# mLSTM head states of both directions in one array, built by zero-padded keys in the pass of the head before

## The chip, the cores and the metric

One core of one Trainium2 chip runs the whole layer. The metric is the device time in microseconds (us) of one execution of the program. The five engines are TensorE (PE; its weight loads are shown as PEld), VectorE (DVE), ScalarE (ACT), GpSimd (POOL) and SyncE (SP); SP issues all DMA transfers of this kernel from one queue, in order.

## The reference, cut to what matters

The layer projects a sequence of 2048 positions, mixes it with two groups of 8 heads each (gated DeltaNet, and mLSTM), and projects back. Everything is float32. The change is in the mLSTM group. Each head runs over the sequence forwards and backwards; in one direction and chunkwise it computes

```python
def step(carry, inp):
    c_state, n_state, m_state = carry
    ...
    num = inter[..., None] * jnp.einsum('bhld,bhde->bhle', q_c, c_state) + jnp.einsum('bhts,bhse->bhte', w_intra, v_c)
    den = inter * jnp.einsum('bhld,bhd->bhl', q_c, n_state) + jnp.sum(w_intra, axis=-1)
    h = num / jnp.maximum(jnp.abs(den), jnp.exp(-m_t))[..., None]
    ...
    c_state = carry_dec[..., None, None] * c_state + jnp.einsum('bhld,bhle->bhde', wk, v_c)
    n_state = carry_dec[..., None] * n_state + jnp.sum(wk, axis=2)
```

A key or query has 64 entries, a value 128. A column of ones behind the values (129 columns, VW) makes n_state and den by the same products as c_state and num.

## The kernel before, in words

The sequence is cut into NC = 16 chunks of 128 positions, and into NB = 4 blocks of CB = 4 chunks. The program has four stages that follow each other, each with pools of its own in SBUF and PSUM: the gates and the first projections; the inversion for the DeltaNet heads woven with the mLSTM projections (m_k, m_q, m_v); the DeltaNet scan; and the mLSTM stage (from line 1188), after which the output projection is finished. In the mLSTM stage PE also does the first half of the output projection for 14 chunks (`ahead`, line 1173, with `product`, line 1161), as filler between the steps of the heads.

Ahead of the mLSTM stage. `gates` makes per-position decay factors; `dec` (line 492) holds the factor by which a state is multiplied from chunk to chunk, for the 16 pairs of direction and head. `m_k` (line 740) transposes the keys, scales them for each direction into `tk` and stores them; `m_v` (line 770) stores the values with their column of ones. Both go into one DRAM array per head, `mwv_d`, whose row of a chunk has 128 entries of keys (64 for each direction) and then 129 of values. So a store writes runs of 512 or 516 bytes, with the other's bytes between them.

The mLSTM stage. `states(h)` (line 1206) walks t = 0 to 15: it loads a block of keys and values together (`wv`, line 1212; 6 buffers), multiplies keys by values in one matmul (`pc`, line 1225; 128 rows of the result: 64 forwards, 64 backwards, for the same chunk t), makes the forward state with one DVE instruction (line 1231), and copies the backward half by ACT into the state array (line 1237). The array `C` has two slots for each chunk, one per direction, with zeros in the half of the partitions that belongs to the other direction. For head h + 1 these steps run inside the pass of head h, one per item; for head 0 they run by themselves at the start of the stage. `pc` has one buffer in PSUM (pool `ps_c`), so the next `pc` waits until both DVE and ACT have read the last.

The pass of a head (`core`, line 1299) takes the chunks from 15 down to 0, an item for each. In an item come, in this order: the backward state of the chunk, in place, by DVE (line 1314); the masking of the next block on POOL every fourth item (`mask_block`, line 1265: two selects on `rb`, and the scaling of the queries `qe`, line 1277); the weights of the next item (`weights`: matmul `pq`, two exponentials on ACT, one product on DVE); one step of `states` for the next head; a stretch of filler; then the matmuls into `pn`: scaled queries times both states in one matmul of 258 columns (line 1335), and weights times values for each direction (line 1339); then the division (lines 1342 to 1346), the sum of the directions (lines 1348 and 1349), and again filler. `load_block` (line 1240) loads keys, queries, `rb` and `qe` two blocks ahead; `qe` is one transfer from two rows of `in_d`, each spread over 64 partitions (line 1259).

The order of PE and of POOL in this stage is the order in which the program is written (`manual_schedule`, line 1363). The other queues (DVE, ACT, SP) are ordered by the framework's planner, which goes by its own model of time; a transfer into a pool is planned no earlier than a buffer of its tag comes free.

## Time and profile before

| what | before |
|---|---|
| median of 3 runs | 2766.45 us (2766.29 to 2770.05) |
| profiled execution, its own time | 2766.64 us |
| its span, first to last instruction | 2764.9 us |
| mean granted TensorE clock | 0.977 of full speed |
| PE, PEld busy | 2574.2 us, 2146.5 us |
| DVE, ACT, POOL busy | 1688.9 us, 1254.8 us, 948.8 us |
| mLSTM stage, first to last of its matmuls | 2112 to 2551 us of the span |

How to read the profile: a busy PE is a PE that has matmuls in flight, not one at its peak. A float32 matmul is two passes, which the trace lists as two instructions; the fillers are one pass. "Idle before" is the time for which an engine had nothing to run, and the arrow names what ended it. The granted clock is given as a share of full speed; its two levels are 1.2 and 2.4 GHz.

### The profile page before, as it was taken

What the parts mean: (1) busy time and instruction counts of PE and PEld (TensorE: products, weight loads), DVE (VectorE), ACT (ScalarE), POOL (GpSimd) and SP (SyncE); (2) the same over time, 40 slices, a digit from 0 to 9 for tenths busy, and PEclk for the clock granted to TensorE, in tenths of its full rate; (3) what the DMA queues carried; (4) which work ended last, traced back from release to release, by engine and by line L of the source; (5) the groups of instructions that cost most, each with busy time, mean ns of one, the idle gap of its engine ahead of it and who ended that gap; (6) DMA issues with size and microseconds to landing.
All of it is one profiled execution on the core that took longest, in us unless ns stands there. A gap on an engine that the chain in (4) does not pass through costs nothing. (4 is left out here: it accounts for less than half of the span.)

```text
span 2764.9 us, 48198 instructions
## 1 busy us (share of the span) xinstructions
PE 2574.2 (93%) x16494; PEld 2146.5 (78%) x16494; DVE 1688.9 (61%) x4176; ACT 1254.8 (45%) x3400; POOL 948.8 (34%) x1410
## 2 busy tenths in 40 slices
PE   7999999999999998999999999999995788889998
PEld 5788878788887776777788888888884677778887
DVE  5547776677768887887425555555554565666333
ACT  6356666666652333433333333333333555555321
POOL 2136665666653232333211111111112333333133
PEclk9999999999999999999999999999997899999999
DMA  4135555655553545454556656666656677775564
GB/s 150 56 101 176 173 168 152 181 157 186 175 181 114 142 117 152 119 150 123 138 158 200 212 183 212 198 211 209 201 172 181 203 211 205 204 208 156 191 190 156
DMA packets 437343, 468.09 MB, mean 169 GB/s; under 512 B 31306, under 2 KB 302570, under 8 KB 437098
## 3 DMA queue, kind: packets, MB, share of 16 engines
q1 hardware_dynamic: 437097, 465.01, 56.3%
q8 instruction: 131, 2.15, 0.3%
q14 instruction: 115, 0.93, 0.1%
HBM read 301.92 MB, written 162.99 MB: 168 GB/s over the span
## 5 line engine op out<-in xcount | busy, mean ns | idle before, releaser
L272 PE MATMUL acc<-hh,wh 128*128 128x512 f32 x2048 | 834.3, 407 | 0.0
L272 PE MATMUL acc<-hl,wh 128*128 128x512 f32 x2048 | 827.6, 404 | 0.0
L272 PE MATMUL acc<-hh,wl 128*128 128x512 f32 x2048 | 822.7, 402 | 0.0
L272 PEld LDWEIGHTS acc<-hh,wl 128*128 128x128 f32 x2048 | 388.6, 190 | 72.8 <-issue 1.0
L272 PEld LDWEIGHTS acc<-hh,wh 128*128 128x128 f32 x2048 | 389.3, 190 | 70.3 <-issue 1.2
L272 PEld LDWEIGHTS acc<-hl,wh 128*128 128x128 f32 x2048 | 389.4, 190 | 69.1 <-issue 1.0
L230 POOL TENSOR_TENSOR wl<-wr,wh 128x256 fp32r<-128x256 f32 x256 | 206.0, 818 | 611.0 <-ACT wh L229 485.0
L579 DVE SCALAR_TENSOR_TENSOR cacc<-raw,gcw,cacc 128x512 f32<-128x512 f32 x256 | 213.4, 860 | 78.1 <-POOL raw L595 37.8
L1167 PE MATMUL po<-woh,ch 128*128 128x512 f32 x512 | 212.6, 416 | 17.6 <-ACT woh L1143 15.6
L150 POOL TENSOR_TENSOR rs<-rs,mhalf 128x4 f32<-128x4 f32 x64 | 64.3, 1010 | 477.0 <-DVE rs L147 232.5
L1167 PE MATMUL po<-wol,ch 128*128 128x512 f32 x512 | 209.7, 410 | 1.4 <-POOL wol L1144 1.4
L1167 PE MATMUL po<-woh,cl 128*128 128x512 f32 x512 | 208.6, 408 | 0.0
L229 ACT CAST wh<-wr 128x256 fp32r<-128x256 f32 (+1 forms) x260 | 98.0, 403 | 235.1 <-DMA wr<-in_w_in_dram 154.1
L710 POOL COPY dg<-T 32x128 f32<-32x128 f32 x256 | 151.9, 593 | 16.6 <-DVE T L700 6.6
L700 DVE SCALAR_TENSOR_TENSOR T<-pk,sc,E 128x256 f32<-128x256 f32 x256 | 109.6, 474 | 47.5 <-PE pk L697 39.6
L874 POOL COPY Z<-ZD 32x256 f32<-32x256 f32 x128 | 92.0, 719 | 123.8 <-DMA Z<-uq_d 68.6
L579 DVE SCALAR_TENSOR_TENSOR cacc<-raw,mcw,cacc 128x512 f32<-128x512 f32 x128 | 100.8, 805 | 52.4 <-POOL raw L595 27.1
L579 DVE SCALAR_TENSOR_TENSOR kq<-raw,gcw,kq 128x512 f32<-128x512 f32 x128 | 104.8, 824 | 33.0 <-ACT kq L575 24.0
L1167 PEld LDWEIGHTS po<-woh,ch 128*128 128x128 f32 x512 | 98.4, 192 | 32.8 <-ACT woh L1143 17.1
L1225 PE MATMUL pc<-wv 128*128 128x129 f32 x256 | 56.9, 317 | 66.8 <-DMA wv<-mwv_d 53.7
L1167 PEld LDWEIGHTS po<-wol,ch 128*128 128x128 f32 x512 | 98.6, 193 | 16.6 <-POOL wol L1144 3.4
L1029 DVE SCALAR_TENSOR_TENSOR sn<-sn,eGL,ps 128x128 f32<-128x128 f32 x224 | 68.0, 344 | 71.1 <-PE ps L1024 71.1
(603 smaller groups left out, 4892.1 us busy)
## 6 DMA issues: line engine op xcount, KB each, us to landing
kv<-kv_d SPq DMA_DIRECT2D x256, 256.0 KB
wr<-in_w_in_dram SPq DMA_DIRECT2D x256, 128.0 KB
uq_d<-T SPq DMA_DIRECT2D x64, 512.0 KB
uq<-uq_d SPq DMA_DIRECT2D x128, 256.0 KB
wv<-mwv_d SPq DMA_DIRECT2D x32, 514.0 KB
zg_d<-zt SPq DMA_DIRECT2D x64, 256.0 KB
E<-grow_d SPq DMA_DIRECT2D x64, 256.0 KB
kv_d<-tk SPq DMA_DIRECT2D x64, 256.0 KB
```

The costliest lines, as they stand in the source:

```text
L150: nc.gpsimd.tensor_tensor(out=rs, in0=rs, in1=mhalf[:, :CB], op=ALU.pow)
L229: nc.scalar.copy(out=hi, in_=raw[:, :, :n])
L230: nc.gpsimd.tensor_tensor(out=lo, in0=raw[:, :, :n], in1=hi.bitcast(F32), op=ALU.subtract)
L272: nc.tensor.matmul(ps, l[:, k % KH, :], r[b][:, k, :], start=(k == 0 and i == 0), stop=(k == KC - 1 and i == 2),)
L579: nc.vector.scalar_tensor_tensor(out=acc, in0=raw[:, t : t + TB], scalar=cw[:, t * n_ct + ct : t * n_ct + ct + 1], in1=acc, op0=ALU.mult, ...
L700: nc.vector.scalar_tensor_tensor(out=T2[d][:, :, i], in0=pk, scalar=sc[:, u, c : c + 1], in1=E[d][:, i].unsqueeze(1).broadcast_to([P, 2, P ...
L710: nc.gpsimd.tensor_copy(out=dg[qs, :, at : at + CB], in_=T2[d][qs, 1, :, qs].rearrange("p c i -> p i c"),)
L874: nc.gpsimd.tensor_copy(out=self.Z[bs, :, :, bs], in_=ZD[bs].rearrange("p x (d c) -> p d c x", d=2)[:, :, self.qs],)
L1029: nc.vector.scalar_tensor_tensor(out=sn[d], in0=st[d], scalar=eGL[:, u, c : c + 1], in1=ps[d][:, 2], op0=ALU.mult, op1=ALU.add,)
L1167: nc.tensor.matmul(po, l[:, i, :], r[:, ns], start=(first and i == 0 and j == 0), stop=(last and i == H - 1 and j == 2),)
L1225: nc.tensor.matmul(pc, wv[:, t % CB, 0:P], wv[:, t % CB, P:], start=True, stop=True)
```

## The change

The states of both directions are made in the pass ahead, by the same instruction. `C` has one slot per step (half the size): slot t holds, in its upper and lower halves of the partitions, the forward state before chunk t and the backward state before chunk 15 - t. For this `pc` is now the sum of two matmuls: the forward keys of chunk t with its values, and the backward keys of chunk 15 - t with its values. Keys are spread into tiles with 64 zeros between the two directions (`wks`), so that a window of 128 columns has the keys of one direction and zeros for the other; POOL spreads them from a staged load. The one DVE instruction then works on 128 partitions, the ACT copy (line 1237) and the in-place backward step (line 1314) are gone, and the step with t = 15 makes no matmul. `dec` is reordered to fit, by 17 POOL copies in `gates`. The scaled queries become two tiles of 128 partitions, each zero in one half, and the matmul of 258 columns becomes two of 129. Keys and values have their own DRAM arrays and loads. Each step of `states` now yields twice: its matmuls stand where they stood, its DVE instruction is emitted later in the item, between lines 1348 and 1349.

```diff
-    mwv_d = [dram.tile([P, NC, 2 * P + 1], F32, name=f"mwv_d{h}") for h in range(H)]
+    mwk_d = [dram.tile([P, NC, 2, 64], F32, name=f"mwk_d{h}") for h in range(H)]
+    mv_d = [dram.tile([P, NC, P + 1], F32, name=f"mv_d{h}") for h in range(H)]
...
-            nc.scalar.activation(out=dec, in_=t2, func=AF.Exp)
+            nc.scalar.activation(out=t2, in_=t2, func=AF.Exp)
+            nc.gpsimd.tensor_copy(out=dec[0:64], in_=t2[0:64, :H])
+            for c in range(NC):
+                nc.gpsimd.tensor_copy(out=dec[64:128, :, c], in_=t2[64:128, H:, NC - 1 - c])
...
-                    nc.sync.dma_start(
-                        out=mwv_d[h][:, cs, 0:P], in_=tk.rearrange("p c d k -> p c (d k)")
-                    )
+                    nc.sync.dma_start(out=mwk_d[h][:, cs], in_=tk)
...
-                nc.sync.dma_start(
-                    out=mwv_d[h][:, b * CB : (b + 1) * CB, P : 2 * P + 1], in_=tk
-                )
+                nc.sync.dma_start(out=mv_d[h][:, b * CB : (b + 1) * CB], in_=tk)
...
-            Cs = [ms.tile([P, NC, 2, VW], F32, name=f"C{i}", bufs=1) for i in range(2)]
+            Cs = [ms.tile([P, NC, VW], F32, name=f"C{i}", bufs=1) for i in range(2)]
             for C in Cs:
-                nc.vector.memset(C[0:64, 0, 0, :], 0.0)
-                nc.vector.memset(C[64:128, NC - 1, 1, :], 0.0)
-                nc.gpsimd.memset(C[0:64, :, 1, :], 0.0)
-                nc.gpsimd.memset(C[64:128, :, 0, :], 0.0)
+                nc.vector.memset(C[:, 0, :], 0.0)
...
+            qes = [ms.tile([P, 2, TB], F32, name=f"qe{i}", bufs=1) for i in range(3)]
+            for qe in qes:
+                nc.gpsimd.memset(qe[64:128, 0, :], 0.0)
+                nc.gpsimd.memset(qe[0:64, 1, :], 0.0)
+            wks = [ms.tile([P, CB, 3, 64], F32, name=f"wk{i}", bufs=1) for i in range(NB)]
+            for wk in wks:
+                nc.gpsimd.memset(wk[:, :, 1, :], 0.0)
+            vs, blk, staged = {}, {}, {}
+            def wk_of(h, b):
+                return wks[b if h % 2 == 0 else (1, 0, 3, 2)[b]]
+            def load_keys(h, blocks):
+                for b in blocks:
+                    t = ms.tile([P, CB, 2, 64], F32, tag="wt", name="wt", bufs=NB)
+                    nc.sync.dma_start(out=t, in_=mwk_d[h][:, b * CB : (b + 1) * CB])
+                    staged[h, b] = t
+            def spread_keys(h, blocks):
+                for b in blocks:
+                    nc.gpsimd.tensor_copy(out=wk_of(h, b)[:, :, ::2, :], in_=staged.pop((h, b)))
+            def load_values(h, blocks):
+                for b in blocks:
+                    vs[h, b] = ms.tile([P, CB, VW], F32, tag="v", name="v", bufs=2 * NB)
+                    nc.sync.dma_start(out=vs[h, b], in_=mv_d[h][:, b * CB : (b + 1) * CB])
...
+                outer, inner = (0, 3), (1, 2)
                 if h == 0:
-                    for b in range(NB):
-                        load(b)
+                    for bs in (outer, inner):
+                        load_keys(0, bs)
+                        load_values(0, bs)
+                        spread_keys(0, bs)
                 for t in range(NC):
-                    if h > 0 and t % CB == 0:
-                        load(t // CB)
...
-                    nc.tensor.matmul(
-                        pc, wv[:, t % CB, 0:P], wv[:, t % CB, P:], start=True, stop=True
-                    )
+                    if h > 0 and t == 0:
+                        load_values(h, inner)
+                        spread_keys(h, inner)
+                    if h + 1 < H and t == NC // 2:
+                        load_keys(h + 1, outer)
+                        load_values(h + 1, outer)
+                    if h + 1 < H and t == NC - CB:
+                        spread_keys(h + 1, outer)
+                        load_keys(h + 1, inner)
+                    if t < NC - 1:
...
+                        for d, c in enumerate((t, NC - 1 - t)):
+                            b, i = c // CB, c % CB
+                            nc.tensor.matmul(
+                                pc, wk_of(h, b)[:, i].rearrange("p s k -> p (s k)")[:, d * 64 : d * 64 + P],
+                                vs[h, b][:, i, :], start=(d == 0), stop=(d == 1),
+                            )
+                    yield
                     if t == 0:
-                        nc.vector.tensor_copy(out=C[0:64, 1, 0, :], in_=pc[0:64])
+                        nc.vector.tensor_copy(out=C[:, 1, :], in_=pc)
                     elif t < NC - 1:
                         nc.vector.scalar_tensor_tensor(
-                            out=C[0:64, t + 1, 0, :], in0=C[0:64, t, 0, :],
-                            scalar=dec[0:64, h, t : t + 1], in1=pc[0:64],
+                            out=C[:, t + 1, :], in0=C[:, t, :], scalar=dec[:, h, t : t + 1], in1=pc,
                             op0=ALU.mult, op1=ALU.add,
                         )
-                    if t > 0:
-                        nc.scalar.copy(out=C[64:128, t - 1, 1, :], in_=pc[64:128])
                     yield
...
-                nc.sync.dma_start(
-                    out=qe,
-                    in_=in_d[h : h + H + 1 : H, bs].unsqueeze(1).broadcast_to([2, 64, TB]),
-                )
+                qe = qes[j % 3]
+                for d in range(2):
+                    nc.sync.dma_start(
+                        out=qe[d * 64 : (d + 1) * 64, d, :],
+                        in_=in_d[d * H + h, bs].partition_broadcast(64),
+                    )
...
-                qv = qe.rearrange("p (c i) -> p c i", i=P)
-                nc.gpsimd.tensor_tensor(out=qv, in0=qv, in1=kq[:, :, 1, :], op=ALU.mult)
+                for d in range(2):
+                    hs = slice(d * 64, (d + 1) * 64)
+                    qv = qe[hs, d, :].rearrange("p (c i) -> p c i", i=P)
+                    nc.gpsimd.tensor_tensor(out=qv, in0=qv, in1=kq[hs, :, 1, :], op=ALU.mult)
...
-                    if c < NC - 2:
-                        nc.vector.scalar_tensor_tensor(
-                            out=C[64:128, c, 1, :], in0=C[64:128, c + 1, 1, :],
-                            scalar=dec[64:128, H + h, c + 1 : c + 2], in1=C[64:128, c, 1, :],
-                            op0=ALU.mult, op1=ALU.add,
-                        )
...
-                    nc.tensor.matmul(
-                        pn, qe[:, i * P : (i + 1) * P], C[:, c], start=True, stop=False
-                    )
-                    for d in range(2):
-                        nc.tensor.matmul(pn[:, d], W[:, d], v, start=False, stop=(d == 1))
+                    for d, slot in enumerate((c, NC - 1 - c)):
+                        nc.tensor.matmul(
+                            pn[:, d], qe[:, d, i * P : (i + 1) * P], C[:, slot, :],
+                            start=True, stop=False,
+                        )
+                        nc.tensor.matmul(pn[:, d], W[:, d], v, start=False, stop=True)
...
                     nc.scalar.activation(out=oc, in_=pn[:, 0, :P], func=AF.Copy, scale=dn[:, 0:1])
+                    next(following, None)
```

## Rows read from the trace of the kernel before

**Rows 1.** Page, part 1: engine, busy us, share of the span, instructions.
```profile
PE 2574.2 (93%) x16494; PEld 2146.5 (78%) x16494; DVE 1688.9 (61%) x4176; ACT 1254.8 (45%) x3400; POOL 948.8 (34%) x1410
```

**Rows 2.** Windows: stretch, length, busy of each engine, PEclk, DMA share, GB/s.
```profile
2100.00:2120.00 20.00, 7.40 (x31) 6.50 (x32) 4.72 (x14) 3.85 (x15) 3.17 (x4) 0.54 0.89 231
...
2325.00:2375.00 50.00, 40.19 (x224) 34.81 (x222) 30.85 (x104) 25.27 (x86) 13.51 (x15) 0.93 0.69 200
```

**Rows 3.** Waits of PE from 2175 to 2510: us in total, times, longest.
```profile
PE pc L1225 <- DMA wv<-mwv_d: 29.5, 12, 3.6
PE pc L1225 <- ACT C L1237: 9.4, 13, 1.7
```

**Rows 4.** Timeline of PE: start, us, line, tiles, count [idle before, and its releaser].
```profile
2175.26 0.60 PE L1335 MATMUL pn<-C,qe 128*128 128x258 f32 x2
...
2185.62 0.60 PE L1335 MATMUL pn<-C,qe 128*128 128x258 f32 x2
...
2316.58 0.60 PE L1335 MATMUL pn<-C,qe 128*128 128x258 f32 x2
2317.01 0.61 PE L1339 MATMUL pn<-wv,W 128*128 128x129 f32 x4
...
2318.15 0.38 PE L1285 MATMUL pq<-kq 128*128 128x128 f32 x2
2318.37 0.39 PE L1225 MATMUL pc<-wv 128*128 128x129 f32 x2
...
2330.19 0.77 PE L1225 MATMUL pc<-wv 128*128 128x129 f32 x2 [3.50 <-DMA wv<-mwv_d]
...
2507.85 0.60 PE L1335 MATMUL pn<-C,qe 128*128 128x258 f32 x2
...
2529.05 0.60 PE L1335 MATMUL pn<-C,qe 128*128 128x258 f32 x2
...
2538.57 0.60 PE L1335 MATMUL pn<-C,qe 128*128 128x258 f32 x2
```

**Rows 5.** Timeline of SP, the queue that issues transfers: start, us to issue.
```profile
2097.01 0.56 SPq L1253 DMA_DIRECT2D rb<-rv_d  x1
2097.62 0.56 SPq L1259 DMA_DIRECT2D qe<-in_d  x1
...
2318.18 3.02 SPq L1212 DMA_DIRECT2D wv<-mwv_d  x1
```

**Rows 6.** Timeline at the start of the mLSTM stage, POOL and PE.
```profile
2102.76 0.63 POOL L1271 TENSOR_SCALAR_AFFINE_SELECT rb<-rb 128x512 f32<-128x512 f32 x1 [4.61 <-DMA rb<-rv_d]
...
2109.96 1.26 POOL L1277 TENSOR_TENSOR qe<-qe,kq 128x512 f32<-128x512 f32 x1 [6.56 <-DMA qe<-in_d]
...
2112.46 7.88 PE L1225 MATMUL pc<-wv 128*128 128x129 f32 x32 [17.57 <-DMA wv<-mwv_d]
```

**Rows 7.** Groups by line, 2175 to 2510: busy us, mean ns | idle before, releasers.
```profile
L1335 PE MATMUL pn<-C,qe 128*128 128x258 f32 x210 | 65.3, 393 | 0.9 <-DVE o L1349 0.9
L1314 DVE SCALAR_TENSOR_TENSOR C<-C,dec 64x129 f32<-64x129 f32 x88 | 36.8, 418 | 3.5 <-ACT C L1237 0.7
L1277 POOL TENSOR_TENSOR qe<-qe,kq 128x512 f32<-128x512 f32 x27 | 35.2, 1305 | 0.0
L1231 DVE SCALAR_TENSOR_TENSOR C<-C,dec,pc 64x129 f32<-64x129 f32 x92 | 30.9, 336 | 24.7 <-PE pc L1225 24.5
L1237 ACT COPY C<-pc 64x129 f32<-64x129 f32 x99 | 25.9, 262 | 33.8 <-DVE C L1231 31.8
L1342 DVE TENSOR_TENSOR dn<-pn,em 128x2 f32<-128x2 f32 x105 | 16.4, 156 | 39.7 <-PE pn L1339 38.9
```

**Rows 8.** Waits from 860 to 1420, of DVE and of PE.
```profile
DVE tk L752 <- DMA mwv_d<-tk: 16.1, 11, 3.0
...
PE pt L604 <- ACT cacc L584: 21.2, 7, 5.9
```

**Rows 9.** Timeline of POOL behind the gates.
```profile
165.53 1.44 POOL L230 TENSOR_TENSOR wl<-wr,wh 128x256 fp32r<-128x256 f32 x2 [19.42 <-ACT wh L229]
```

More of the change, by code (lines that the diff above doesn't have):

```diff
@@ L107 @@
     wkc = cols.tile([P, U, NC], F32, name="wkc")
-    dec = cols.tile([P, U, NC], F32, name="dec")
+    dec = cols.tile([P, H, NC], F32, name="dec")
     em = cols.tile([P, U, NC], F32, name="em")
@@ L1206, in states @@
+            def load_values(h, blocks):
+                for b in blocks:
+                    vs[h, b] = ms.tile([P, CB, VW], F32, tag="v", name="v", bufs=2 * NB)
+                    nc.sync.dma_start(out=vs[h, b], in_=mv_d[h][:, b * CB : (b + 1) * CB])
             def states(h):
                 C = Cs[h % 2]
-                def load(b):
-                    wvs[h, b] = ms.tile([P, CB, P + VW], F32, tag="wv", name="wv", bufs=6)
-                    nc.sync.dma_start(out=wvs[h, b], in_=mwv_d[h][:, b * CB : (b + 1) * CB, :])
+                outer, inner = (0, 3), (1, 2)
@@ L1214, in states @@
                 if h == 0:
-                    for b in range(NB):
-                        load(b)
+                    for bs in (outer, inner):
+                        load_keys(0, bs)
+                        load_values(0, bs)
+                        spread_keys(0, bs)
                 for t in range(NC):
-                    if h > 0 and t % CB == 0:
-                        load(t // CB)
-                    wv = wvs[h, t // CB]
-                    if h == 0 and t % 3:
-                        pc = ps_n.tile([P, 2, VW], F32, tag="pn", name="pc")[:, 0]
-                    else:
-                        pc = ps_c.tile([P, VW], F32, tag="pc", name="pc")
@@ new lines, in states @@
+                    if t < NC - 1:
+                        if h == 0 and t % 3:
+                            pc = ps_n.tile([P, 2, VW], F32, tag="pn", name="pc")[:, 0]
+                        else:
+                            pc = ps_c.tile([P, VW], F32, tag="pc", name="pc")
+                        for d, c in enumerate((t, NC - 1 - t)):
[4 more added lines that the diff above has]
+                            )
@@ L1303, in core @@
                 load_block(0)
-                for _ in states(0):
-                    yield
+                for i, _ in enumerate(states(0)):
+                    if i % 2:
+                        yield
                 mask_block(0)
@@ L1332, in core @@
                     i = c % CB
[L1333 removed]
+                    qe, v = blk[h, b][1], vs[h, b][:, i, :]
                     pn = ps_n.tile([P, 2, VW], F32, tag="pn", name="pn")
[L1335 to L1339 removed]
+                    for d, slot in enumerate((c, NC - 1 - c)):
[4 more added lines that the diff above has]
+                        nc.tensor.matmul(pn[:, d], W[:, d], v, start=False, stop=True)
                     dn = ms.tile([P, 2], F32, tag="dn", name="dn")
```

3 lines of the change are left out of this document (removed).

## The prediction

> **What bounds the kernel now.** I read the busy shares first: PE 93%, DVE 61%, ACT 45%, POOL 34% [rows 1]. That would say that more matmuls cost their full length and that work taken from DVE and ACT gives nothing. The share is a mean over four stages, though, so I read the stage that the change touches. In the windows of the mLSTM stage PE is busy 40.2 of 50 us, at 0.93 of its clock, DVE 30.9, ACT 25.3, POOL 13.5, the transfers 0.69 [rows 2]: no engine is full there. So the third view is what PE waits for in the regular part, from 2175 to 2510: 29.5 us in 12 waits of pc for the block wv of keys and values, and 9.4 us in 13 waits of pc for the ACT copy that still holds its one PSUM buffer [rows 3]. Nothing else there is near them.
>
> The timeline of PE gives the price of an item without waits. From 2175.26 to 2185.62 four items take 10.36 us, 2.59 each, and PE goes from one matmul to the next. The pn matmuls of the stretch number 105 (210 passes [rows 7]), from 2175.26 to 2507.85, so 104 items take 332.6 us, 3.20 each [rows 4]. At 10.36 for four they would take 269.4; 63.2 us are lost, of which the two waits are 38.9. The other 24.3 are PE at the lower clock behind waits (0.93 in the window), smaller waits, and some fillers more than the 20 in my four items.
>
> Why wv is late: its load was issued at 2318.18, the issue alone took 3.02 us [rows 5], and the matmul that needs it began at 2330.19, after a wait of 3.50 us [rows 4]. That is 12.0 us from issue to use, against some four items (10.4 us) for which a free buffer leads its use, six buffers holding one and a half heads. The lead is short, not the engine.
>
> **The change part by part.** The sum is made on the profiled execution, 2766.6 us; the median of the runs is 0.2 below it, so I take them as one.
>
> - *Wait for wv.* Values get eight buffers (two heads). With the pass going from chunk 15 down, the buffers of one head come free after its items 3, 7, 11 and 15, and go to blocks that are needed at steps 0 and 4 of the states two heads on: leads of 5 to 13 items, 14 us or more, against 12.0. Staged keys come free as soon as POOL has spread them, eight items and more ahead. So the wait goes: -29.5. What is late next I put at +5 (below).
> - *Wait for the ACT copy.* The copy (262 ns, behind exponentials on its queue [rows 7]) is gone; pc is free after one DVE instruction: -9.4.
> - *Lower clock behind these waits.* Of the 24.3 us I give half back: -12 (between 0 and -18).
> - *Matmuls added.* A step had one pc and has two, but none at t = 15: 30 for 16 per head, 98 more for the seven heads inside the passes. Items without states (head 7, 2529.05 to 2538.57) take 9.52 us for four, with the same 20 fillers and one group of transposes as the 10.36 above: a pc costs 0.84/4 = 0.21 us [rows 4]. That is +20.6 us, all on PE, where nothing hides it. The split of pn's 258 columns: two passes took 0.43 (2316.58 to 2317.01), two passes of 128 columns 0.22 (2318.15 to 2318.37) [rows 4]; 0.44 for 0.43, times 128 items, +1.3.
> - *DVE and ACT.* The in-place step (418 ns, 88 in the stretch) goes, and the other keeps its 336 ns with twice the partitions, since the length along them is the same [rows 7]. Both engines were off the path, so this gives nothing beyond the waits above.
> - *POOL.* Scaling qe becomes two instructions of the same length: 1305 ns more for each of 32 blocks [rows 7]. The 32 spreads have no row; by the rows of 512 columns they lie between 0.63 [rows 6] and 1.31; I take 1.0. In a head that is 4 x (1.3 + 1.0) = 9.2 us more, over some 45 us in which POOL was a quarter busy [rows 2]. Hidden by that idle time; if a spread has to wait for its keys, the masks behind it in POOL's order wait too, and that is a rival below. The large zeroings of C go and smaller ones come: POOL was done with them before the data came.
> - *Copies of dec.* 17 small POOL copies behind the gates. POOL stood idle for 19.4 us up to 165.53 [rows 9]; 17 at no more than 0.6 (an estimate: the select of 512 columns takes 0.63) are 10: 0, at worst +2.
> - *New waits.* SP issues 64 transfers more (qe in two, keys and values apart) at some 0.5 us [rows 5], two more for every four items, and the same bytes in a shorter time: 0.69 x 3.20/2.85 = 0.77 of the transfer engines. I take +5; bounds 0 and +29.5, which is the old wait again.
> - *Start of the stage.* PE waits 17.6 us for wv to begin [rows 6]. Now its first step needs blocks 0 and 3, twice the bytes: 514 KB more at 231 GB/s [rows 2] is +2.2, a spread +1.0, 14 more pc of head 0 +2.9. Against that: rb, issued at 2097.01, is used at 2102.76, 5.75 us later; qe, as large, was issued 0.61 us after it and is used at 2109.96, 12.3 us later [rows 5, 6], and wv, queued behind it, at 2112.46. The new qe loads have the form of rb's, one row over many partitions. If they land as rb does, all behind them gains 12.3 - 5.75 = 6.6. Between -6.6 and +6.1; I take -3. The Trainium skill ("DMA: Bandwidth & Descriptors", section "Why a DMA increments its semaphore by 16 and not by 1") says that a transfer is split over as many of the 16 engines as divide the slowest dimension of both its sides; two rows spread over 64 partitions each would get two. The rows of rb and qe agree with it, though they don't show engines. The same page of the Trainium skill, in its rules for kernel authors, says that two transfers to the two partition halves gain nothing over one of 128 partitions; by that, the start would cost +6. The first would hold for each of 32 blocks, and its result is the first rival.
> - *Stores ahead.* DVE waits 16.1 us for stores of keys from 860 to 1420, and PE 21.2 us for the convolved tiles that DVE makes [rows 8]. Runs of 512 bytes become runs of 2 KB; if that halves the store, part of DVE's wait passes on to PE. Between -16 and +2 (the planner may reorder); near nothing, as most of PE's waits have no such wait in front: -3.
>
> Sum: 2766.6 - 29.5 - 9.4 - 12 + 20.6 + 1.3 + 5 - 3 - 3 = 2736.6, say 2737.
>
> **The rivals.**
> 1. *Transfers land much sooner.* It is qe's form that holds up the transfers behind it, in every block, as it did at the start [rows 5, 6]. Then the start gains 6.6 for each of its first two blocks (-13.2), there is no new wait, and the lower clock gives 18: 2766.6 - 29.5 - 9.4 - 18 + 21.9 - 13.2 - 3 = 2715. For it: 12.0 us for a wv of 514 KB, where 200 GB/s need 2.6. Against it: in the regular part the queue is 0.69 busy anyway.
> 2. *The keys are late in place of wv (slower).* Keys now go from DRAM to POOL to PE, and POOL's order is fixed: a spread that waits for its load holds up the masks, these the exponentials, and these PE. It decides if a staged load takes more than the four items between its place in the program and the spread's, 11.4 us, which it does if the load is issued there and not ahead and takes wv's 12.0. Then the wv waits stay under other names, with their clock, and only the ACT copy's goes: 2766.6 + 21.9 - 9.4 = 2779. Against it: the loads of before were issued as soon as a buffer was free, ahead of their place.
> 3. *pc is freed too late.* The DVE step is emitted behind the reciprocal of the item. If DVE runs in that order, pc is free only after the end of pn, three small instructions of 0.156 and one of 0.336: 0.80 us. From the end of pn (2317.01 + 0.61) to the next pc (2318.37) is 0.75 [rows 4, 7]. So each of 98 steps waits at least 0.05, and at most the 0.72 that a wait for the ACT copy took (9.4/13); with 0.3, +29: 2766. Against it: the planner gives DVE what is ready, and the DVE step is ready before pn is.
>
> **How the numbers follow.** The forecast 0.55 (its own range 2722 to 2752); rival 1 0.20, rival 2 0.12, rival 3 0.13. A measurement of this kernel tells 0.2%, 5.5 us, from no change: faster is below 2760.9, slower above 2772. The forecast gives 0.52 faster, 0.02 the same, 0.01 slower; rival 1 0.20 faster; rival 2 0.12 slower; rival 3 0.06, 0.05 and 0.02. Together 0.78, 0.07 and 0.15. The range of 8 in 10, 2705 to 2768, leaves out rival 2, the upper end of rival 3 and the lowest of rival 1.
>
> **What would show it.** Right: no wait of pc for a load in the regular part, no wait of pc for ACT or DVE; items near 2.59 + 0.21 x 14/16 = 2.77 us; PE's busy share in these windows up and its clock near 1. Rival 1: first pc before 2106. Rival 2: pc waits for POOL, or POOL's spreads for their loads. Rival 3: pc waits for the DVE step in most items. The forecast is wrong if items stay at 3.2 us, or if the time is lost in another stage, which only the planner could cause.

## The result and the profile after

The changed kernel takes 2704.07 us (median; 2702.86 to 2706.48) where the kernel before takes 2768.25 us on the same chip (2766.29 to 2771.01): a ratio of 0.9769, with a 95% interval from 0.9752 to 0.9785. The forecast was 2737, the range 2705 to 2768. The sign was right; the gain was over twice the size, and the time lies 1 us beyond the range's lower end. The profiled execution took 2702.94 us with a span of 2701.1, against a span of 2764.9 before.

Part 1 of the page after (columns as in [rows 1]):

```profile
PE 2572.4 (95%) x16974; PEld 2165.6 (80%) x16974; DVE 1646.5 (61%) x4062; ACT 1215.4 (45%) x3280; POOL 1008.8 (37%) x1497
```

PE has 480 instructions more and is busy 1.8 us less; the mean granted clock over the span is 0.984 where it was 0.977. To find where the 63.8 us of span went I cut both spans at four marks that both timelines of PE have: the first pv that reads AXn (stage 2 begins), the last transposes of vt (stage 2 ends), the last transposes of ob (the scans end), and the last pn that reads C. The marks of the changed kernel, in its timeline of PE:

```profile
868.01 0.47 PE L859 MATMUL pv<-AXn,Z 32*32 32x32 f32 x32 [2.14 <-DVE AXn L848]
...
1400.06 0.60 PE L609 MATMUL pt<-ident,vt 128*128 128x128 f32 x4
...
2075.39 1.03 PE L161 MATMUL pt<-ident,ob 128*128 128x128 f32 x8
...
2487.65 0.39 PE L1365 MATMUL pn<-C,qe 128*128 128x129 f32 x2
```

and of the kernel before:

```profile
866.73 0.65 PE L858 MATMUL pv<-AXn,Z 32*32 32x32 f32 x32 [3.51 <-DVE AXn L847]
...
1417.00 0.60 PE L604 MATMUL pt<-ident,vt 128*128 128x128 f32 x4
...
2093.85 1.03 PE L160 MATMUL pt<-ident,ob 128*128 128x128 f32 x8
...
2550.76 0.60 PE L1335 MATMUL pn<-C,qe 128*128 128x258 f32 x2
```

| stretch | before | after | difference |
|---|---|---|---|
| up to stage 2 | 866.7 | 868.0 | +1.3 |
| stage 2, 868 to 1400 | 550.3 | 532.0 | -18.2 |
| scans | 676.8 | 675.3 | -1.5 |
| mLSTM stage | 456.9 | 412.3 | -44.6 |
| the rest | 214.1 | 213.4 | -0.7 |

So two places gained, and one of them, stage 2, holds none of the new matmuls. In the mLSTM stage two windows (columns as in [rows 2]), the start of the stage and its regular part:

```profile
2080.00:2100.00 20.00, 9.62 (x66) 9.29 (x66) 5.18 (x15) 0.00 (x0) 3.06 (x5) 0.66 1.04 265
2300.00:2350.00 50.00, 50.00 (x354) 45.92 (x353) 30.60 (x114) 26.48 (x93) 25.56 (x29) 1.00 0.81 232
```

In the regular part PE is busy 50.0 of 50 us at a clock of 1.00, against 40.19 at 0.93 [rows 2]; the transfers go from 0.69 to 0.81 and from 200 to 232 GB/s. The answer to [rows 3], all waits of PE from 2150 to 2450, is one line:

```profile
PE po L1168 <- POOL wol L1145: 0.7, 1, 0.7
```

PE's timeline over the same items as in [rows 4] (k = 7, k = 111, and between them four items in a row):

```profile
2089.78 2.52 PE L1257 MATMUL pc<-v,wk 128*128 128x129 f32 x9 [13.36 <-POOL wk L1224]
...
2150.49 0.38 PE L1365 MATMUL pn<-C,qe 128*128 128x129 f32 x2
...
2153.65 0.39 PE L1365 MATMUL pn<-C,qe 128*128 128x129 f32 x2
...
2164.97 0.39 PE L1365 MATMUL pn<-C,qe 128*128 128x129 f32 x2
...
2445.84 0.38 PE L1365 MATMUL pn<-C,qe 128*128 128x129 f32 x2
```

From 2150.49 to 2445.84 the 104 items take 295.35 us, 2.84 each, where they took 332.6. Four items with one group of transposes take 11.32 us (2153.65 to 2164.97) against 10.36 before [rows 4]: in this group the added matmuls cost 0.24 us an item against my 0.20. The groups of 2150 to 2450 that answer to [rows 7]:

```profile
L1365 PE MATMUL pn<-C,qe 128*128 128x129 f32 x424 | 81.8, 274 | 0.0
L1311 POOL TENSOR_TENSOR qe<-qe,kq 64x512 f32<-64x512 f32 x54 | 71.7, 1328 | 2.0
L1265 DVE SCALAR_TENSOR_TENSOR C<-C,dec,pc 128x129 f32<-128x129 f32 x93 | 32.1, 346 | 3.8 <-PE pc L1257 2.8
L1224 POOL COPY wk<-wt 128x512 f32<-128x512 f32 x24 | 14.0, 612 | 0.0
```

POOL's scaling of half the partitions takes as long as one of all (1328 ns for 1305), a spread 612 ns and not my 1.0 us, and DVE's step on 128 partitions 346 ns for 336 on 64. All of this is hidden.

### The profile page after: what moved, and what is told of

Its sections match the earlier page's. It is cut to its first block, busy times and chain, and to the rows that moved or that the text cites. A ratio compares the mean times of both kernels' runs of the same rounds, so it can differ in the third digit from the quotient of the medians.

```text
span 2701.1 us, 49253 instructions
## 1 busy us (share of the span) xinstructions
PE 2572.4 (95%) x16974; PEld 2165.6 (80%) x16974; DVE 1646.5 (61%) x4062; ACT 1215.4 (45%) x3280; POOL 1008.8 (37%) x1497
## 4 chain that ended last, share of the span: by engine, by line
PE 60%; DVE 11%; DMA 10%; issue 10%; POOL 6%; ACT 3%; SPq 1%; POOLq 0%; DVEq 0%; ACTq 0%
PE acc L273 32%; PE po L1168 5%; DVE cacc L584 3%; DMA E<-grow_d 2%; PE ps L1002 2%; PE pn L1369 2%; DMA kv<-kv_d 2%; PE pn L1365 2%; DVE dm L829 2%; DVE tmp L825 2%; PE ps L993 2%; PE ps L1025 2%; PE po L1039 2%; PE po L1038 2%; PE pc L1257 2%
## 5 line engine op out<-in xcount | busy, mean ns | idle before, releaser
L1168 PE MATMUL po<-woh,ch 128*128 128x512 f32 x512 | 210.3, 411 | 14.3 <-ACT woh L1144 13.5
L1369 PE MATMUL pn<-v,W 128*128 128x129 f32 x512 | 101.2, 280 | 8.1 <-DVE W L1327 8.0
```

Source lines behind the costliest of these rows:

```text
L1168: nc.tensor.matmul(po, l[:, i, :], r[:, ns], start=(first and i == 0 and j == 0), stop=(last and i == H - 1 and j == 2),)
L1369: nc.tensor.matmul(pn[:, d], W[:, d], v, start=False, stop=True)
```

## The experiments

Twelve kernels ran. The marks are those of the table above; "stage 2" and "mLSTM stage" are those two stretches of each kernel's profiled run. Each ratio is to the kernel before on the same chip. A stage is read from one profiled run; those of e2, e7 and e9 took 8, 9 and 13 us more than the median of their kernel, that of e13 10 us less, so that differences of a few us between stages say little.

| run | ratio, 95% interval | stage 2 | mLSTM stage |
|---|---|---|---|
| before (profiled run) | 1 | 550.3 | 456.9 |
| after | 0.9769 [0.9752, 0.9785] | 532.0 | 412.3 |
| e1_arrays_apart | 0.9982 [0.9964, 1.0001] | 531.9 | 476.7 |
| e2_arrays_joint | 0.9845 [0.9823, 0.9867] | 550.2 | 412.7 |
| e3_qe_two | 0.9799 [0.9776, 0.9822] | 549.3 | 403.2 |
| e4_wv_early | 0.9998 [0.9982, 1.0014] | 548.5 | 457.9 |
| e7_qe_cols | 1.0044 [1.0025, 1.0063] | 549.6 | 474.6 |
| e8_apart_qe_two | 0.9811 [0.9791, 0.9831] | 532.8 | 419.1 |
| e9_apart_qe_two_pc2 | 0.9812 [0.9775, 0.9849] | 534.6 | 426.9 |
| e10_after_qe_one | 1.0031 [1.0012, 1.0050] | 533.4 | 486.9 |
| e11_step_early | 0.9754 [0.9741, 0.9766] | 534.2 | 409.6 |
| e12_blocked_qe_two | 0.9726 [0.9711, 0.9741] | 535.3 | 402.4 |
| e13_blocked | 0.9935 [0.9918, 0.9953] | 527.2 | 453.7 |
| e14_blocked_qe_two_dve | 0.9721 [0.9707, 0.9735] | 533.8 | 398.4 |

### Was it the load of qe, or the lead of the values?

**e3_qe_two**: the kernel before, with one edit.

```diff
-                nc.sync.dma_start(
-                    out=qe,
-                    in_=in_d[h : h + H + 1 : H, bs].unsqueeze(1).broadcast_to([2, 64, TB]),
-                )
+                for d in range(2):
+                    nc.sync.dma_start(
+                        out=qe[d * 64 : (d + 1) * 64, :],
+                        in_=in_d[d * H + h, bs].partition_broadcast(64),
+                    )
```

> The kernel before with one edit: each qe tile is loaded by two transfers, one row spread on 64 partitions each, in place of one transfer with a 2x64x512 source. Theory C (the slow landing of qe holds the wv transfer behind it on the queue): qe lands in about 4-5 us, the first pc comes 5-7 us earlier, TensorE's waits for wv between 2175 and 2510 fall from 29.5 to under 5 us, items fall from 3.15 to about 2.85 us, the kernel reads 2725-2740 us. Rival D (the wv tile comes late because its buffer is freed late, and a deeper supply of values is what after gained): the waits for wv stay above 20 us and the kernel reads 2755-2768 us.

Measured: 2716.88 us, before 2771.33. The mLSTM stage falls by 53.7 us, more than the whole change gained there. Its waits of PE from 2160 to 2460:

```profile
PE pc L1225 <- ACT C L1237: 12.6, 15, 1.9
PE pn L1336 <- DVE dn L1344: 1.2, 1, 1.2
PE pn L1336 <- DVE o L1350: 0.9, 1, 0.9
```

The wait for wv is gone, with the same six buffers and the same order of the program. Theory C holds and its gain is larger than expected. qe's landing, which the trace of before does not give, is 4.1 us (median) here.

**e4_wv_early**: the kernel before, the load of each wv written two items earlier in the program.

```diff
...
-                    if h > 0 and t % CB == 0:
-                        load(t // CB)
+                    if h > 0 and t % CB == 2 and t // CB + 1 < NB:
+                        load(t // CB + 1, h)
+                    if h + 1 < H and t == NC - 2:
+                        load(0, h + 1)
```

> The kernel before with one edit: each wv tile is loaded two items earlier in the order of the program, out of the same six buffers; qe as before. Theory D (lead of the values): waits for wv between 2175 and 2510 fall from 29.5 to under 8 us and the kernel reads 2735-2748 us. Theory C (queue held by qe): the transfer is issued earlier but two items are 6 us, so the waits fall by at most half, to 12-25 us, and the kernel reads 2752-2765 us.

Measured: 2771.93 us against 2771.33, no change. Waits of PE from 2179 to 2515:

```profile
PE pc L1227 <- DMA wv<-mwv_d: 24.1, 12, 3.8
PE pc L1227 <- ACT C L1239: 8.6, 12, 1.5
PE pc L1227 <- ACT E L1290: 5.6, 5, 1.4
```

The time fits neither theory's forecast, because the edit did not reach the queue. Behind the scans this run issues its 427 transfers in the order of the kernel before, but for two near the start, and from the issue of a wv to its first matmul it is 11.3 us in both runs (median over heads 1 to 7). So e4 does not test theory D; that the waits for wv are 24.1 us for 29.5, and those for E 5.6 for 1.9, shows how far two runs of nearly one order differ. What speaks against a short lead is e3: there it is 9.9 us from issue to first matmul, shorter than before, and no wait for wv is left.

What is ahead of a wv on the queue is seen in the view of the transfers in slices, of the kernel before from 2314 to 2334 (40 slices of 0.5 us; the first line is the busy share of the 16 DMA engines in tenths, the second GB/s). The wv of [rows 5] is issued at 2318.18, behind a qe (2317.07) and the store of a zt:

```profile
DMA  1019898899999949679999971111111398995699
GB/s 49 37 57 270 295 377 266 340 385 311 213 200 234 292 136 163 113 257 366 341 271 279 270 238 49 49 46 52 49 45 62 102 307 291 356 262 162 211 237 258
```

For seven or eight slices, from about 2326 to 2330, 0.1 of the engines are busy and they move 49 GB/s; elsewhere up to 385 are moved. A sixteenth of 385 is 24, and two engines of sixteen are 0.125 of them: this is what two engines at their full rate give while fourteen stand. The window of that stretch in the kernel before (columns as in [rows 2]):

```profile
2326.00:2330.00 4.00, 0.69 (x5) 0.41 (x3) 0.90 (x4) 1.06 (x3) 0.00 (x0) 0.99 0.16 57
```

PE is busy 0.69 of 4 us: the whole core all but stands until qe has gone through and wv, behind it, lands for the pc at 2330.19 [rows 4]. That is 256 KB (the page's size of a qe) at 49 GB/s, 5.3 us, an estimate from these rows, 32 times; the mLSTM stage lost 53.7 us by it (e3). In the run with qe in two, the same view from 2296 to 2316:

```profile
DMA  9985002899959999655998999988479999798999
GB/s 430 394 164 110 0 0 90 245 303 250 112 156 292 345 349 217 139 213 217 348 393 258 205 235 314 299 345 271 150 265 288 282 290 175 227 298 350 356 271 266
```

Here no slice has the 0.1 with 49 GB/s; the only hole is one where nothing was issued.

The issuing queue stands behind qe as well. SP issues in order, and its load of zt waits for the store cat_d<-zt that was issued right behind qe. Its waits for this store, in the kernel before from 2175 to 2510 and in e3 from 2160 to 2460 (columns as in [rows 3]):

```profile
SPq L152 <- DMA cat_d<-zt: 144.0, 25, 7.2
...
SPq L152 <- DMA cat_d<-zt: 18.0, 17, 3.0
```

So SP stands for 144.0 of 335 us, and with qe in two for 18.0 of 300. What is behind a qe lands late, and what is behind that is issued late; what each of the two is worth was not separated.

**e7_qe_cols**: is it that there are two transfers, or that each has one row? The kernel before, qe in two transfers cut by columns, so that each still has two rows outermost.

```diff
+                for n in range(2):
+                    ns = slice(n * TB // 2, (n + 1) * TB // 2)
                     nc.sync.dma_start(
-                        out=qe,
-                        in_=in_d[h : h + H + 1 : H, bs].unsqueeze(1).broadcast_to([2, 64, TB]),
+                        out=qe[:, ns],
+                        in_=in_d[h : h + H + 1 : H, bs][:, ns].unsqueeze(1).broadcast_to([2, 64, TB // 2]),
                     )
```

> The kernel before with qe loaded by two transfers, but cut by columns: each still has two rows spread on 64 partitions each (source 2x64x256). Theory C1 (a transfer whose slowest dimension is two moves on two of the engines, whatever its size): the stretches in which the transfers fall to about 50 GB/s at a busy share of 0.1 stay, the waits of TensorE for wv between 2175 and 2510 stay at 25-30 us, the kernel reads 2760-2772 us. Theory C2 (two transfers are faster than one because they are two): it reads as the cut by rows did, 2710-2725 us.

Measured: 2784.54 us against 2773.5, slower. The view of the transfers from 2314 to 2334:

```profile
DMA  1115996999988999976289111111119189999769
GB/s 47 47 47 184 379 184 170 345 370 348 252 168 150 254 365 374 181 160 134 79 261 293 52 48 38 47 47 49 47 49 165 46 271 395 370 363 260 119 150 279
```

The same stretches at mostly 47 to 49 GB/s, only longer; the time is above both theories' forecasts. So it is the form of the transfer, two rows in its slowest dimension, not the count.

The Trainium skill ("DMA: Bandwidth & Descriptors", section "Why a DMA increments its semaphore by 16 and not by 1") has the rule: the number of engines is the largest, up to 16, that divides the slowest dimension of both sides. The busy share of 0.1 and the 49 GB/s agree with it. By the other rule that I weighed, of the same page of the Trainium skill, two transfers to the two halves gain nothing; the 54 us of e3 say that it does not hold where the one transfer has two rows outermost.

**e10_after_qe_one**: the kernel after, with qe's factors loaded by one transfer again, into a staging tile from which POOL scales.

```diff
-            qes = [ms.tile([P, 2, TB], F32, name=f"qe{i}", bufs=1) for i in range(3)]
+            qes = [ms.tile([P, 2, TB], F32, name=f"qe{i}", bufs=1) for i in range(2)]
...
+            qss = [ms.tile([P, TB], F32, name=f"qs{i}", bufs=1) for i in range(2)]
...
-                for d in range(2):
-                    nc.sync.dma_start(
-                        out=qe[d * 64 : (d + 1) * 64, d, :],
-                        in_=in_d[d * H + h, bs].partition_broadcast(64),
-                    )
+                nc.sync.dma_start(
+                    out=qss[j % 2],
+                    in_=in_d[h : h + H + 1 : H, bs].unsqueeze(1).broadcast_to([2, 64, TB]),
+                )
...
-                    nc.gpsimd.tensor_tensor(out=qv, in0=qv, in1=kq[hs, :, 1, :], op=ALU.mult)
+                    qs = qss[j % 2][hs].rearrange("p (c i) -> p c i", i=P)
+                    nc.gpsimd.tensor_tensor(out=qv, in0=qs, in1=kq[hs, :, 1, :], op=ALU.mult)
```

> The kernel after with one edit: the inter-chunk row factors come by one transfer of two rows spread on 64 partitions each into a staging tile, from which GpSimd scales into the zero-padded qe (qe and staging two buffers each). Theory C1 (the form of this transfer is what slowed before): TensorE waits for v, keys or kq return between 2150 and 2450, 25 us or more, the start of the stage is 6 us longer, the kernel reads 2735-2765 us. Rival D (the eight value buffers and keys staged apart hide any late transfer): no such wait, 2702-2712 us.

Measured: 2778.98 us against 2773.5, above the range expected: the whole gain is gone, though stage 2 keeps its 17 us (533.4). The longest waits of PE and of SP from 2190 to 2500:

```profile
PE pc L1258 <- DMA v<-mv_d: 40.9, 6, 10.1
...
SPq L153 <- DMA cat_d<-zt: 102.6, 23, 8.5
```

and the window:

```profile
2190.00:2500.00 310.00, 268.85 (x1801) 245.24 (x1800) 158.09 (x589) 140.97 (x483) 144.98 (x158) 0.93 0.66 189
```

With eight value buffers, two heads of them, and staged keys, PE still waits up to 10.1 us at a time for values, and its clock is 0.93 again. The buffers do not give the lead that I expected of them: with SP standing 102.6 us for the same store, the last of a head's four loads of values is issued between 0.2 us before and 3.0 us after the start of the step that needs it (heads 3 to 7), where it is 11.5 us or more ahead in the changed kernel. Joint states with this load cost 30 us more than separate ones (486.9 against 456.9); the edit also leaves qe two buffers in place of three, and no run tells the two apart.

### Stage 2: the stores

**e1_arrays_apart** and **e2_arrays_joint** do and undo the form of the stores, and change the loads with it.

```diff
# e1, from the kernel before
+    mwk_d = [dram.tile([P, NC, 2, 64], F32, name=f"mwk_d{h}") for h in range(H)]
+    mv_d = [dram.tile([P, NC, P + 1], F32, name=f"mv_d{h}") for h in range(H)]
...
+                    nc.sync.dma_start(out=mwk_d[h][:, cs], in_=tk)
...
+                nc.sync.dma_start(out=mv_d[h][:, b * CB : (b + 1) * CB], in_=tk)
...
+                    nc.sync.dma_start(
+                        out=wvs[h, b][:, :, :P].rearrange("p c (d k) -> p c d k", d=2),
+                        in_=mwk_d[h][:, b * CB : (b + 1) * CB],
+                    )
+                    nc.sync.dma_start(
+                        out=wvs[h, b][:, :, P:], in_=mv_d[h][:, b * CB : (b + 1) * CB]
+                    )
# e2, from the kernel after
+    mwv_d = [dram.tile([P, NC, 2 * P + 1], F32, name=f"mwv_d{h}") for h in range(H)]
...
+                    nc.sync.dma_start(
+                        out=mwv_d[h][:, cs, 0:P], in_=tk.rearrange("p c d k -> p c (d k)")
+                    )
...
```

> The kernel before with one edit: weighted keys and values are stored to two DRAM arrays (runs of 2048 and 2064 bytes per partition) and each wv tile of the last stage is loaded by two transfers into the same tile. Theory A (the form of the stores alone made stage 2, from the first pv at 868 us to the last transposes, shorter by 18 us): stage 2 falls from 550 to 531-534 us, the wait of VectorE for its tk buffers behind the stores falls from 16 to about 7 us, the kernel reads 2745-2753 us. Rival B (stage 2 gained through something else that the change reordered): stage 2 stays at 547-552 us and the kernel at 2764-2772 us. In the last stage the waits of TensorE for wv stay (about 29 us between 2175 and 2510), since the load of qe and the number of wv buffers are as before.

> The kernel after with one edit undone: keys and values go back into one DRAM array (runs of 512 and 516 bytes per store), and the last stage loads each by its own transfer out of it. Theory A (form of the stores): stage 2 goes back from 532 to 549-552 us, the kernel from 2704 to 2720-2726 us with the last stage as in after. Rival B: stage 2 stays at 532 us. If the last stage also slows by more than 5 us, the runs of 512 bytes of its loads matter too.

Measured: e1 2766.54 against 2771.33, in sum hardly to be told from no change, but its stage 2 takes 531.9 us; e2 2730.0 against 2771.33 (4 us above the range expected), its stage 2 550.2. Theory A holds both ways. e1 gives the 18 us back in the mLSTM stage (+20), where each wv now comes by two transfers that write pieces of 512 and 516 bytes into a strided tile; this price I had not expected. In e2 the last stage stays as in after (412.7 for 412.3), although its loads read pieces of 512 and 516 bytes too, into tiles of their own and with more buffers. So short pieces alone are not e1's price; pieces, the count of transfers and buffers were not separated.

The order of the instructions in stage 2 is the same in all of these kernels. What the stores change there, in the view of the queues (packets, MB, share of the 16 engines), is in the kernel before, from 866.7 to 1417,

```profile
q1 hardware_dynamic: 88019, 71.93, 47.1%
```

and in the kernel after, from 868 to 1400,

```profile
q1 hardware_dynamic: 63832, 71.94, 42.7%
```

24,187 packets less for the same bytes, and a smaller share of a shorter stage. The waits in the kernel after, 860 to 1403, answer to [rows 8]:

```profile
DVE tk L757 <- DMA mwk_d<-tk: 7.2, 5, 3.3
...
PE pt L609 <- ACT cacc L589: 19.8, 6, 5.6
```

DVE's wait for the stores of keys falls from 16.1 to 7.2; the wait of PE that I had looked at hardly moves (21.2 to 19.8). The larger rows are POOL's, for the stores of values: `tv`, the tile they read, has its three buffers in common with `raw`, a tile of the convolution. Before (860 to 1420) and after (860 to 1403):

```profile
POOL raw L592 <- DMA mwv_d<-tv: 52.2, 5, 15.8
POOL raw L594 <- DMA mwv_d<-tv: 29.2, 6, 12.0
...
POOL raw L597 <- DMA mv_d<-tv: 31.7, 4, 13.5
```

With its smaller rows POOL waits 95.4 us for stores of values before and 44.0 after, 76 to 78 in e2 and e3 (short pieces) and 52 to 58 in e1, e12 and e13 (long ones). What of it reaches PE is spread over many small waits: of the 18 us, PE's idle time gives 11.6 (37.0 to 25.4 us) and its busy time 6.7 (513.3 to 506.6 us), at 0.97 of its clock for 0.96.

**e13_blocked** asks whether it takes two arrays or only long runs: one array, in which each block holds its key columns and then its value columns; wv by one transfer.

```diff
-    mwv_d = [dram.tile([P, NC, 2 * P + 1], F32, name=f"mwv_d{h}") for h in range(H)]
+    mwv_d = [dram.tile([P, NB, CB * (2 * P + 1)], F32, name=f"mwv_d{h}") for h in range(H)]
...
-                        out=mwv_d[h][:, cs, 0:P], in_=tk.rearrange("p c d k -> p c (d k)")
+                        out=mwv_d[h][:, cs.start // CB, 0 : CB * P],
+                        in_=tk.rearrange("p c d k -> p (c d k)"),
...
-                    nc.sync.dma_start(out=wvs[h, b], in_=mwv_d[h][:, b * CB : (b + 1) * CB, :])
+                    nc.sync.dma_start(out=wvs[h, b], in_=mwv_d[h][:, b])
...
```

> The kernel before with the blocked layout alone (qe by one transfer as before): if the length of runs is what stage 2 gained, 532 us there as with two arrays, and the last stage as before (457 us, waits for wv 25-30 us): 2746-2754 us. If two arrays are what it takes, 550 us and 2764-2772 us.

Measured: 2755.0 us against 2773.09; stage 2 527.2 us, the waits for wv stay (24.6 us from 2160 to 2495). The runs are what counts: 2048 and 2064 bytes in place of 512 and 516. Over all runs stage 2 takes 527 to 535 us with long runs and 548 to 550 with short ones.

### What the joint states are worth

**e8_apart_qe_two** is the sum of e1 and e3; **e9_apart_qe_two_pc2** adds a second buffer for pc, at the cost of one of pq.

```diff
-            ps_c = st_.enter_context(tc.tile_pool(name="ps_c", bufs=1, space=PSUM, reuse_waits="tile"))
-            ps_q = st_.enter_context(tc.tile_pool(name="ps_q", bufs=2, space=PSUM, reuse_waits="tile"))
+            ps_c = st_.enter_context(tc.tile_pool(name="ps_c", bufs=2, space=PSUM, reuse_waits="tile"))
+            ps_q = st_.enter_context(tc.tile_pool(name="ps_q", bufs=1, space=PSUM, reuse_waits="tile"))
```

> The kernel before with two edits alone: keys and values stored to two arrays (wv loaded by two transfers into one tile) and qe loaded by two transfers, one row each. Matmuls, states and buffers as before. If the gains are those two forms of transfers and add up (-18 in stage 2, -54 by qe): 2694-2704 us, as fast as after or faster, since after has 98 + 128 matmuls more and e3 keeps 12.6 us of waits for the ACT copy against them. If the second wv transfer costs here what it cost without the qe edit (the last stage 20 us longer): 2712-2722 us.

> As the kernel with the two forms of transfers, and pc gets two PSUM buffers (pq one). If the wait of pc for the ACT copy is a matter of its one buffer: the 12.6 us of waits between 2160 and 2460 fall to under 3, and the kernel is 8-14 us below that one (2682-2694 us). If one pq buffer costs as much (matmuls of pq wait for W of the item before): waits of pq appear and the time is the same within 5 us.

Measured: e8 2721.54 and e9 2720.35, against 2773.5. In e8 stage 2 gains its 18 us and the last stage gives 16 of them back (419.1 against e3's 403.2), as e1 did: the gains do not add up with wv by two transfers in short pieces. With wv by one transfer they do (402.4 in e12, below). In e9 the 11.9 us for the ACT copy vanish from 2170 to 2470, and others take their place (the longest rows; this run took 13 us more than the median of its kernel):

```profile
PE pc L1228 <- ACT E L1292: 6.4, 3, 2.5
PE pc L1228 <- DMA wv<-mv_d: 5.6, 4, 2.7
PE pn L1339 <- DVE o L1353: 5.0, 5, 1.9
PE pc L1228 <- DMA qe<-in_d: 3.5, 1, 3.5
PE pq L1289 <- DVE W L1297: 3.4, 4, 1.3
```

**e12_blocked_qe_two** is e13 with e3's load of qe: only the two forms of transfers, no joint states. **e14_blocked_qe_two_dve** also moves the copy out of pc from ACT to DVE. **e11_step_early** is the kernel after with the state's DVE step written right behind its matmuls.

```diff
# e14, beside e12's edits
-                        nc.scalar.copy(out=C[64:128, t - 1, 1, :], in_=pc[64:128])
+                        nc.vector.tensor_copy(out=C[64:128, t - 1, 1, :], in_=pc[64:128])
# e11, from the kernel after
-                    yield
                     if t == 0:
                         nc.vector.tensor_copy(out=C[:, 1, :], in_=pc)
...
-                    next(following, None)
```

> The kernel before with two edits in the layout of transfers alone: one DRAM array as before, but each block of it holds its 512 key columns and then its 516 value columns, so that stores have runs of 2048 and 2064 bytes and wv comes by one transfer of 4112 bytes a partition; and qe by two transfers of one row each. If the second wv transfer with its short pieces was what the arrays apart lost in the last stage: stage 2 532 us, last stage 403 us, together 2694-2702 us, below after by 2 to 10 us: the joint states then are worth nothing or less. If it reads 2712 us or more, the gains of the two forms do not add up for another reason.

> As the blocked layout with qe in two, and the copy of the reverse state's product out of pc goes to VectorE in place of ScalarE. VectorE is 0.73 busy there, ScalarE 0.65. If the 12.6 us of waits of pc for the ACT copy come from ScalarE's queue (exponentials ahead of it): they fall below 4 us and the kernel is 5-10 us faster. If VectorE's queue is no shorter, the wait moves to VectorE and the time is the same within 4 us.

> The kernel after with one edit undone: the VectorE step of a state is emitted right behind its matmuls and not behind the reciprocal of the item. Theory E (the planner puts the step where it is ready, or VectorE has room anyway): no wait of pc, within 3 us of after (2702-2708 us). Rival 3 of the prediction turned round (the place of the step in VectorE's order decides when pc is free): pc waits for VectorE appear or change by 5 us or more.

Measured, all three on one chip, before 2773.09: e12 2697.76, e14 2695.29, e11 2704.82. The planner gave e11 the same order as after, on every engine, so that it says only that the place of that step in the text is nothing, and serves as a second measurement of after, beside e12. e12 is 7 us faster than it, each of its runs (2691.37 to 2700.97) below each of e11's (2702.08 to 2710.57), and the fastest with e14. The waits of PE in e12, 2145 to 2440, its window, and its first pc and the items k = 7 and k = 111 in PE's timeline:

```profile
PE pc L1226 <- ACT C L1240: 13.0, 16, 1.9
PE pn L1339 <- DVE o L1353: 0.9, 1, 0.9
```

```profile
2145.00:2440.00 295.00, 280.87 (x1688) 245.49 (x1686) 215.37 (x769) 195.25 (x659) 121.17 (x134) 1.00 0.84 237
```

```profile
2092.32 4.04 PE L1226 MATMUL pc<-wv 128*128 128x129 f32 x15 [10.97 <-DMA wv<-mwv_d]
...
2147.04 0.60 PE L1339 MATMUL pn<-C,qe 128*128 128x258 f32 x2
...
2441.17 0.60 PE L1339 MATMUL pn<-C,qe 128*128 128x258 f32 x2
```

e12 still has the 13.0 us for the ACT copy that joint states remove, at a clock of 1.00, and its mLSTM stage takes 402.4 us against 412.3 in after and 409.6 in e11. Little of that is lost in the items: from k = 7 to k = 111 e12 takes 294.1 us, after and e11 295.4. There joint states take away 13.9 us of waits and bring about 15 us of matmuls, an estimate from these times. The rest is lost at the start, by joint states and what they bring with them (keys and values apart, the spread, twice the matmuls of pc): from the last transposes of the scans to k = 7 it is 66.7 us in e12, 75.1 in after and 72.4 in e11 (63.7 in e3 and 66.7 in e14, which have no joint states; 75.6 in e2, which has them). The first pc comes 12.0 us behind these transposes in e12 and 14.4 and 14.3 in the others, and head 0 has 60 passes of pc ahead of its first pn in place of 32; how much each costs was not separated. In e14 the wait is 10.1 us for DVE in place of 13.0 for ACT, and the times overlap: inconclusive, with medians 2.5 us apart.

## Why the prediction was wrong

The sum forecast 30.0 us, the profiled runs differ by 63.7. Of the 33.7 us missed, 15.2 are in the stores ahead, 10.6 in the items from k = 7 to 111, 3.3 in the start, and 4.6 in what is left of the program. By its steps:

- **The wait for wv, -29.5.** The size was right, the cause was wrong, and this is the step that failed first. "The lead is short, not the engine" falls with e3: the form of qe's load, with unchanged buffers and a lead of 9.9 us for 11.3, gives the whole of it. Eight buffers do not remove the wait in e10, and e4 says nothing on it. I had the true cause as rival 1 and set against it that "in the regular part the queue is 0.69 busy anyway". That 0.69 is a mean of slices of 0.9 and slices of 0.1, and the slices were there to be seen.
- **The lower clock, -12, and the new waits, +5.** Of the 63.2 us that the items had lost 37.2 came back, and 15 to 25 more were spent on matmuls (below); no wait was new: rival 1's -18 and 0 were nearer. From k = 7 to 111 the change gave 37.2 us; my terms over the same 104 items come to 26.6 (29.5 + 9.4 + 12, less 19.1 + 1.1 for 91 matmuls of pc and the split of pn, less 4.1 of the new waits).
- **Matmuls, +21.9.** Right, as far as the runs tell: over the 104 items I had 20.2; the group of four says 25 (0.24 an item), e12 against after about 15.
- **The wait for the ACT copy, -9.4.** Right that it goes. e12 shows that its price in matmuls is as large, and that the start loses 6 to 8 us more.
- **The start, -3.** The wait of the first pc falls from 17.57 to 13.36 us, now behind a spread; from the last transposes of the scans to k = 7 it takes 75.1 us for 81.4, -6.3, near my bound of -6.6. The first pc came 14.4 us behind these transposes, where it came 18.6. With qe in two alone (e3) this stretch takes 63.7 us, -17.7: the two new loads gave more than I had allowed, and joint states took most of it back.
- **Stores ahead, -3.** The most mis-sized term: -18.2, beyond my bound of -16. I read one wait, DVE's 16.1 us for the stores of keys, and left out POOL's 95.4 us for the stores of values, which fall to 44.0. The 21.2 us of PE that I set beside it are waits for a step of ACT, not of DVE [rows 8], and hardly move.
- **Rivals 2 and 3.** No pc waits for POOL or for DVE in the regular part. The planner puts the step where it is ready, as was argued against rival 3; e11 shows that its place in the program has no say in it.

Rival 1's 2715, with the stores at -18 in place of -3, is 2700; measured 2703 in the profiled run. Part of this agreement is luck, since its start was -13.2 and measured -6.3; its items are right (-36.7 by its terms, measured -37.2). So the likeliest case was chosen wrong, and the stores then took the time past the lower end.

## What to carry to other kernels

When transfers come late, cut the view of the transfers into slices before you ask for more buffers: a busy share of 0.1 at a constant 49 GB/s, between slices of 0.9, was here a transfer that ran on two engines and held back all behind it, and two transfers of one row each undid it for 2% of this kernel's time. A mean share of a stage cannot show this; the waits of the issuing queue can. When an experiment moves a transfer in the program, read from the trace whether its issue moved. Lay out what a pass stores for a later pass so that each store and each load has one long run to a partition: blocks by turns gave both (e12, with qe in two) and beat the kernel that was rebuilt around them by 7 us, so take the cheap edits out of a large change and time them by themselves.

## What was not expected of the hardware

- Pieces of 512 and 516 bytes in stores are slow enough here to matter: in 2-KB runs the same data saved 18 us of a stage of 550 in which the queue was only 0.47 busy.
- Loading wv by two transfers into a strided tile (pieces of 512 and 516 bytes on the side of the SBUF) in place of one costs 16 to 20 us over the last stage, whether the queue is held by qe (e1) or not (e8). Whether the pieces or the count of transfers do it was not tested.
- One transfer cut by columns into two, with two rows outermost in each, is slower than the one: 2784.54 against 2773.5 us.
- What remains open: why the first pc still comes 11.8 us behind the scans with qe in two (e3), and what the start of the changed kernel loses against e12.
